# Prompt attention by pairs of heads, and a later gather of the sample values, in a hybrid decoder layer

## The chip, the cores and the metric

The kernel runs on one core of a Trainium2 chip. The metric is device time in microseconds (us) of one execution, the median over several runs; lower is better. The engines of the core are called PE (TensorE: matrix products, with PEld for its loads of the stationary operand), DVE (VectorE), ACT (ScalarE), POOL (GpSimd) and SP (SyncE, which here only issues DMAs). SBUF is the on-chip memory of 128 rows, PSUM the accumulators that PE writes.

## The reference, cut to what matters

One layer works on 1024 prompt tokens and on 8 samples of 4 tokens each (1056 columns in all). It projects the normalised input to queries, keys and values of 8 attention heads of width 64, to the inputs of a gated delta rule with 4 heads of width 128, and to two gates; it runs both branches, merges them under the gates, and ends with an MLP. The change touches the prompt part of this branch:

```
def stick_breaking(q, k, v, q_pos, k_pos, sb_bias):
    z = einsum('bqhd,bkhd->bhqk', q, k) * d ** -0.5 + sb_bias      # 8 heads, d = 64
    mask = k_pos[None, :] < q_pos[:, None]
    log_1m = where(mask, log_sigmoid(-z), 0)
    suffix = cumsum(log_1m, axis=3, reverse=True) - log_1m
    w = where(mask, exp(log_sigmoid(z) + suffix), 0)               # beta * product of (1 - beta) behind it
    return einsum('bhqk,bkhd->bqhd', w, v)
```

and, for the samples, the place where the pages of the cached keys and values (256 past tokens of each sample, two pages of 128) are gathered from a pool by a page table.

## The kernel before

**Products.** Results have to be exact to about fp32, and PE's fast format is float32r, so an operand is kept as a high and a low part. A dense product is three float32r products, of weights high by input high, weights high by input low, weights low by input high: lines L137, L138 and L139, wherever they appear. `tr` (L111) transposes a 128x128 block through PE.

**Order.** The program is written stage by stage, and a scheduler sets the order of each engine's instructions from its own simulated times. `tc.issue_after(x)` keeps what is written inside it behind instruction x, and `tc.high_priority()` lifts it ahead. Tiles come from pools with a number of buffers per tag; a PSUM tile is one bank of 128x512, from four pools: `dtile`, `gtile`, `ttile`, and a flag of `dtile` for a small fourth one.

**Stages.** Input projection and the prompt's delta-rule heads come first (0 to 520 us of the profile). Then the samples' delta rule (pool `dk`; it lies roughly at 545 to 600 us) and the samples' attention. From about 658 to 907 us comes the prompt's stick-breaking attention, and the MLP fills the rest.

**Sample keys and values.** For each sample s, `keys(s)` gathers two key pages into `kg` (L594, GpSimd's indirect DMA of 128 rows by 512 numbers) and transposes them on PE (`dkt`); `values(s)` gathers two value pages into `vg` (L607). They are called in turn for samples 0 to 3, ahead of the samples' delta rule. That rule multiplies keys and queries with the samples' stored states, two batches of 32 products into `dks` (L723: `sst` state against `kz` masked keys; each uses all rows and 32 columns of the array), and solves a small triangular system; `dMT` is its transposed matrix, `drk` (POOL, L114) a norm that `ds` (DVE, L702) needs. `dst` (L766) are the updates of the states.

**Prompt attention.** A block is one head `hh` and one tile `i` of 128 queries; it sees n = 128 (i+1) keys. For a head, `attn_load` puts q high into rows 0 to 63 and q low into rows 64 to 127 of `qs`, and key high twice into `kh`, key low twice into `kl`. The scores of a block are then two products of the whole array's 128 rows for each 512 keys, `sc<-kh,qs` (L932) and `sc<-kl,qs` (L933), which make all four of high by high, high by low, low by high and low by low. ACT's sigmoid (L934) empties PSUM into `s`; POOL masks the diagonal (L935) and forms `am` = 1 - s (L938); DVE makes the running product `pr` (L942) and multiplies (L943). PE transposes the weights (`wt<-ident,s`, L111), ACT copies them out (L954), and PE multiplies with the values: `po<-wt,vn` (L980 and L994), each with 64 columns of the array, so that 128 rows by 64 columns work. For heads 0 to 5 one `po` tile holds two query tiles of one head, one in each half of the columns, and ACT copies it to `oT` (L982), written out once per head. For heads 6 and 7 one `po` tile holds both heads, and its result stays in SBUF.

The pipeline runs blocks in order; at block x it issues the scores of block x + LAG (LAG = 4), then the transposes of block x (behind those scores by `issue_after`), then fill work, then the values of x. Fill work in the first SPLIT = 34 blocks is the gate projection `pd_g` and the residual's transposes `xrp`, and in the rest the products `pb` of the other branch. Heads 6 and 7 go from the longest block to the shortest.

Of the kernel before, what the change touches and what calls it, by code (L numbers as in the profile page):

```python
# [18 lines left out]
P = 128  # L19
D = 1024  # L20
NP = 1024
# [9 lines left out]
HD = 64  # L31
GH = 4
NC = NP // P
# [5 lines left out]
def hybrid_step(ctx, tc, x_prompt, x_sample, cache_k, cache_v, page_table, state_conv, state_ssm,  # L39
# [5 lines left out]
    V, S_, G, PE, SY = nc.vector, nc.scalar, nc.gpsimd, nc.tensor, nc.sync  # L45
# [132 lines left out]
    blk = keep.tile([P, 32, 4], F32, name="blk")  # L178
# [13 lines left out]
    for t in range(9):  # L192
        n = P if t < 8 else NS
# [9 lines left out]
        for hf in range(2):  # L203
            pt = (ttile, gtile)[hf](f"xtp{t}_{hf}")
# [374 lines left out]
    bk = pool("bk", stack=bctx, side="right")  # L579
    idx = bk.tile([P, 16], I32, name="idx")  # L580
# [6 lines left out]
    cvf = cache_v[0].rearrange("n t h d -> (n t) (h d)")  # L587

    vgs, kts_ = {}, {}
# [14 lines left out]
    def values(s):  # L604
        vgs[s] = bk.tile([P, 2, 512], F32, tag="vg", name=f"vg{s}", bufs=4)
        for pg in range(2):
            G.indirect_dma_start(vgs[s][:, pg, :], None, cvf, bass.IndirectOffsetOnAxis(ap=idx[:, 2 * s + pg:2 * s + pg + 1], axis=0))  # L607

    for s in range(4):
        keys(s)  # L610
        values(s)
    dctx = ExitStack()
    dk = pool("dk", stack=dctx, side="right")
    blkf = blk.rearrange("p b t -> p (b t)")
# [10 lines left out]
                    channel_multiplier=0)  # L625
# [14 lines left out]
    for b in range(3):  # L640
        pt = gtile(f"cvo{b}")
# [70 lines left out]
    pmt = gtile("dmt")  # L712
    tr(pmt[:, 0:P], dM)
    dMT = dk.tile([P, P], F32, name="dMT")
    V.tensor_copy(dMT, pmt[:, 0:P])
    pks = gtile("dks")
    for i, i0 in enumerate((4, 0)):
        kz = dk.tile([P, GH, NSEQ, NS], F32, tag="big", name=f"kz{i}")
# [2 lines left out]
        for s in range(NSEQ):  # L721
            for h in range(GH):
                PE.matmul(pks[32 * h:32 * h + 32, i * P:(i + 1) * P], lhsT=kz[:, h, s, :], rhs=sst[:, s, h, :],  # L723
                          start=(s == 0), stop=(s == NSEQ - 1))
# [6 lines left out]
    for it in range(3):  # L731
# [21 lines left out]
                           op0=ALU.mult, op1=ALU.mult)  # L753
# [8 lines left out]
    for hf in range(2):  # L762
        pts = [(gtile if h % 2 == 0 else ttile)(f"dst{h}{hf}") for h in range(GH)]
# [85 lines left out]
    for g in range(2):  # L849
# [5 lines left out]
        for s4 in range(4):  # L855
            s = 4 * g + s4
# [47 lines left out]

    actx = ExitStack()
    ak = pool("ak", 2, stack=actx, side="right")
    LAG = 4

    def attn_load(hh):
        p, a = hh // 2, hh % 2  # L910
        rs = slice(64 * a, 64 * a + 64)
        qs = ak.tile([P, NP], F32R, tag="qs", name=f"qs{hh}")
        kh = ak.tile([P, NP], F32R, tag="kh", name=f"kh{hh}")
        kl = ak.tile([P, NP], F32R, tag="kl", name=f"kl{hh}")

        for r in range(2):
            hs = slice(64 * r, 64 * r + 64)
            SY.dma_start(qs[hs].bitcast(F32), q_d[r][p, rs])
            SY.dma_start(kh[hs].bitcast(F32), k_d[0][p, rs])
            SY.dma_start(kl[hs].bitcast(F32), k_d[1][p, rs])  # L920
        return qs, kh, kl

    def scores(blk):
        hh, i = blk
        qs, kh, kl = heads[hh]
        n = P * (i + 1)
        qsl = slice(i * P, n)
        s = ak.tile([P, NP], F32, tag="s", name=f"s{hh}_{i}", bufs=LAG + 2)
        for k0 in range(0, n, 512):
            kn_ = min(512, n - k0)  # L930
            pt = dtile(f"sc{hh}_{i}_{k0}")
            PE.matmul(pt[:, :kn_], lhsT=qs[:, qsl], rhs=kh[:, k0:k0 + kn_], start=True, stop=False)  # L932
            last = PE.matmul(pt[:, :kn_], lhsT=qs[:, qsl], rhs=kl[:, k0:k0 + kn_], start=False, stop=True)  # L933
            S_.activation(s[:, k0:k0 + kn_], pt[:, :kn_], AF.Sigmoid, bias=sbb[:, hh:hh + 1], scale=HD ** -0.5)  # L934
        G.affine_select(s[:, qsl], s[:, qsl], pattern=[[-1, P]], compare_op=ALU.is_gt, fill=0.0, base=0,  # L935
                        channel_multiplier=1)
        am = ak.tile([P, NP], F32, tag="am", name=f"am{hh}_{i}", bufs=2)
        G.tensor_scalar(am[:, :n], s[:, :n], -1.0, 1.0, op0=ALU.mult, op1=ALU.add)  # L938

        pr = ak.tile([P, NP], F32, tag="pr", name=f"pr{hh}_{i}")  # L940
        am_r = am[:, n - 1:0:-1]
        V.tensor_tensor_scan(pr[:, n - 1:0:-1], am_r, am_r, 1.0, op0=ALU.mult, op1=ALU.bypass)  # L942
        V.tensor_tensor(s[:, :n - 1], s[:, :n - 1], pr[:, 1:n], op=ALU.mult)  # L943
        return s, last

    def transposed(blk, s):
        hh, i = blk
        wt = ak.tile([P, NP], F32, tag="wt", name=f"wt{hh}_{i}", bufs=2)
        for b0 in range(0, i + 1, 4):
            bn = min(4, i + 1 - b0)  # L950
            pt = ttile(f"wt{hh}_{i}_{b0}")
            for b in range(bn):
                tr(pt[:, b * P:(b + 1) * P], s[:, (b0 + b) * P:(b0 + b + 1) * P])
            S_.activation(wt[:, b0 * P:(b0 + bn) * P], pt[:, :bn * P], AF.Copy)  # L954
        return wt

    heads, vns, oTs, wts = {}, {}, {}, {}

    def load_v(p):
        vn = ak.tile([P, NC, P], F32, tag="vn", name=f"vn{p}", bufs=2)  # L960
        SY.dma_start(vn, v_d[p])
        return vn

    def values_of(blk):
        hh, i = blk
        p, a = hh // 2, hh % 2
        vn = vns[p]
        if hh < 6:
            if i % 2 == 0:
                return  # L970
            m = i // 2
            if m == 0:
                oTs[hh] = ak.tile([P, NC // 2, P], F32, tag="oT", name=f"oT{hh}")
            rs = slice(64 * a, 64 * a + 64)
            po = gtile(f"po{hh}_{m}")
            for b in range(2 * m + 2):
                for r in range(2):
                    if b > 2 * m + r:
                        continue
                    PE.matmul(po[64 * r:64 * r + 64, 0:P], lhsT=vn[:, b, rs], rhs=wts[hh, 2 * m + r][:, b * P:(b + 1) * P],  # L980
                              start=(b == 0), stop=(b == 2 * m + r))
            S_.activation(oTs[hh][:, m, :], po[:, 0:P], AF.Copy)  # L982
            if m == NC // 2 - 1:
                for r in range(2):
                    SY.dma_start(o_d[p, rs, 0:NP].rearrange("d (m r c) -> d r m c", r=2, c=P)[:, r],
                                 oTs[hh][64 * r:64 * r + 64])
            return
        if a == 0:
            return
        po = gtile(f"po6_{i}")  # L990
        for b in range(i + 1):
            for x in range(2):
                rs = slice(64 * x, 64 * x + 64)
                PE.matmul(po[rs, 0:P], lhsT=vn[:, b, rs], rhs=wts[6 + x, i][:, b * P:(b + 1) * P], start=(b == 0), stop=(b == i))  # L994
        cs_ = slice(i * P, (i + 1) * P)
# [3 lines left out]
    blks = [(hh, i) for hh in range(6) for i in range(NC)] + [(6 + a, i) for i in range(NC - 1, -1, -1) for a in range(2)]  # L999
    NB = len(blks)  # L1000
    SPLIT = 34
    state = {}

    def stage_a(x):
        if x >= NB:
            return
        hh, _ = blks[x]
        if hh not in heads:
            if hh // 2 not in vns:
                vns[hh // 2] = load_v(hh // 2)  # L1010
            heads[hh] = attn_load(hh)
        state[x] = scores(blks[x])

    def stage_b(x, fill):

        ahead = state[min(x + LAG, NB - 1)][1]
        with tc.issue_after(ahead.ins):
            wts[blks[x]] = transposed(blks[x], state[x][0])
        for f in fill:
            f()  # L1020
# [122 lines left out]
    pipeline(SPLIT, NB - 2, steps[:-6])  # L1143
    pipeline(NB - 2, NB, steps[-6:])
# [518 lines left out]
```

## Time and profile before

| what | value |
|---|---|
| median of 3 runs | 1745.47 us (1745.25 to 1745.96) |
| profiled execution | 1754.63 us, of which the span is 1752.9 us |
| granted TensorE clock, mean | 0.992 |
| PE busy | 1704.8 us, 97% of the span, 13902 products |
| DVE, ACT, POOL busy | 1148.9, 783.2, 206.6 us |

The profiled execution is 9.2 us longer than the median. Busy times in the views are of that execution. A row of a timeline gives start, duration, engine, line, operation, output and operands, array shape, and how often it runs in succession; a bracket gives the idle time before it and what ended it. Since products overlap in the pipeline, what one product costs is the distance from its start to the next start, and not its duration.

### The profile page before, as it was taken

The numbers are of one execution on the slowest core, as the hardware profiler recorded it, in microseconds if no ns is written. First come the engines' busy times: TensorE is split into PE (matmuls) and PEld (weight loads), VectorE is DVE, ScalarE is ACT, GpSimd is POOL, SyncE is SP. The second block draws the span as 40 slices with busy tenths as digits, with TensorE's granted clock in tenths as the row PEclk, the third lists the DMA queues.
The fourth block names the chain that finished last, engine by engine and source line by source line (L and its number), as shares of the span: only waits on it lengthen the run. The fifth ranks groups of instructions, "written<-read, shape, count | busy, mean of one in ns | idle before, by whom it ended". The sixth has DMA issues, their size and how long they took to land.

```text
span 1752.9 us, 34523 instructions
## 1 busy us (share of the span) xinstructions
PE 1704.8 (97%) x13902; PEld 1645.2 (94%) x13902; DVE 1148.9 (66%) x2299; ACT 783.2 (45%) x1554; POOL 206.6 (12%) x247
## 2 busy tenths in 40 slices
PE   7999999999998999999999999999999999999998
PEld 6999999999998787887989999999999999999998
DVE  6665677868224416658857487887777678788843
ACT  5553435343323225555433355554544564444353
POOL 1110111110004125335310000000000000000000
PEclk9999999999998999999999999999999999999999
DMA  5142232234337457758223644554443666532321
GB/s 177 37 127 67 67 117 79 81 96 144 118 97 230 138 161 210 188 145 248 67 86 117 194 126 146 164 150 148 146 150 133 212 215 220 170 123 90 128 83 66
DMA packets 234219, 239.22 MB, mean 136 GB/s; under 512 B 22882, under 2 KB 192195, under 8 KB 234060
## 3 DMA queue, kind: packets, MB, share of 16 engines
q1 hardware_dynamic: 229110, 226.27, 42.4%
q0 software_dynamic: 3200, 10.52, 1.9%
q8 instruction: 109, 1.79, 0.4%
q10 hardware_dynamic: 1750, 0.23, 0.1%
q14 instruction: 50, 0.41, 0.1%
HBM read 163.21 MB, written 73.77 MB: 135 GB/s over the span
## 4 chain that ended last, share of the span: by engine, by line
PE 74%; issue 8%; DMA 6%; DVE 6%; POOL 3%; ACT 1%; SPq 1%; POOLq 0%; DVEq 0%; ACTq 0%
PE pu L139 6%; PE pu L137 6%; PE pu L138 6%; PE pw L139 4%; PE pw L138 4%; PE pw L137 4%; PE pd_g L137 2%; POOL am L938 2%; PE pd_g L139 2%; PE pd_g L138 2%; POOL s L935 1%; PE px L138 1%; PE px L137 1%; PE px L139 1%; PE pv L137 1%
## 5 line engine op out<-in xcount | busy, mean ns | idle before, releaser
L139 PE MATMUL pu<-Xh,ul 128*128 128x264 f32 x812 | 230.1, 284 | 0.0
L137 PE MATMUL pu<-Xh,uh 128*128 128x264 f32 x812 | 229.8, 283 | 0.1
L138 PE MATMUL pu<-Xl,uh 128*128 128x264 f32 x812 | 229.7, 283 | 0.0
L137 PE MATMUL pw<-hc,w 128*128 128x264 f32 x728 | 205.4, 285 | 2.4 <-ACT w L1475 2.4
L138 PE MATMUL pw<-hc,w 128*128 128x264 f32 x728 | 205.7, 286 | 0.0
L139 PE MATMUL pw<-hc,w 128*128 128x264 f32 x728 | 200.9, 285 | 1.0 <-DVE w L1476 1.0
L137 PEld LDWEIGHTS pu<-Xh,uh 128*128 128x128 f32 x812 | 153.1, 189 | 0.3 <-ACT uh L1226 0.3
L137 PE MATMUL pd_g<-xh,wh_g 128*128 128x256 f32 (+1 forms) x512 | 150.9, 295 | 1.8 <-ACT gt L1037 1.6
L138 PEld LDWEIGHTS pu<-Xl,uh 128*128 128x128 f32 x812 | 152.7, 188 | 0.0
L139 PEld LDWEIGHTS pu<-Xh,ul 128*128 128x128 f32 x812 | 152.0, 188 | 0.0
L139 PE MATMUL pd_g<-xh,wl_g 128*128 128x256 f32 (+1 forms) x512 | 149.2, 291 | 0.1
L138 PE MATMUL pd_g<-xl,wh_g 128*128 128x256 f32 (+1 forms) x512 | 148.6, 290 | 0.0
L137 PEld LDWEIGHTS pw<-hc,w 128*128 128x128 f32 x728 | 137.9, 190 | 2.6 <-ACT w L1475 2.6
L138 PEld LDWEIGHTS pw<-hc,w 128*128 128x128 f32 x728 | 137.2, 189 | 0.0
L139 PEld LDWEIGHTS pw<-hc,w 128*128 128x128 f32 x728 | 134.4, 188 | 1.4 <-DVE w L1476 1.4
L942 DVE TENSOR_TENSOR_SCAN pr<-am 128x127 f32<-128x127 f32 (+7 forms) x64 | 88.1, 1378 | 54.8 <-POOL am L938 54.8
L137 PEld LDWEIGHTS pd_g<-xh,wh_g 128*128 128x128 f32 x512 | 97.8, 191 | 7.0 <-ACT gt L1037 3.0
L139 PEld LDWEIGHTS pd_g<-xh,wl_g 128*128 128x128 f32 x512 | 97.6, 191 | 2.0 <-issue 1.9
L138 PEld LDWEIGHTS pd_g<-xl,wh_g 128*128 128x128 f32 x512 | 97.6, 191 | 0.6 <-issue 0.4
L1475 ACT ACTIVATE w<-a 128x512 fp32r<-128x512 f32 x78 | 43.5, 620 | 84.5 <-PE pw L139 74.4
L139 PE MATMUL px<-mh,wl_wo 128*128 128x264 f32 x256 | 72.2, 285 | 0.9 <-DVE wl_wo L1227 0.8
L138 PE MATMUL px<-ml,wh_wo 128*128 128x264 f32 x256 | 72.6, 285 | 0.0
(584 smaller groups left out, 5126.2 us busy)
## 6 DMA issues: line engine op xcount, KB each, us to landing
hc_d<-t SPq DMA_DIRECT2D x26, 924.0 KB
hc<-hc_d SPq DMA_DIRECT2D x87, 264.0 KB
a<-in_w_down_dram SPq DMA_DIRECT2D x48, 256.0 KB
ws_g<-in_w_in_dram SPq DMA_DIRECT2D x16, 512.0 KB
ws_wo<-in_w_o_dram SPq DMA_DIRECT2D x32, 256.0 KB
ua<-in_w_up_dram SPq DMA_DIRECT2D x16, 512.0 KB
ub<-in_w_up_dram SPq DMA_DIRECT2D x16, 512.0 KB
gA_d<-gt SPq DMA_DIRECT2D x8, 528.0 KB
```

Source lines behind the costliest of these rows:

```text
L137: PE.matmul(pt[:, :n], lhsT=wh[k], rhs=xh[k], start=(k == 0), stop=False)
L138: PE.matmul(pt[:, :n], lhsT=wh[k], rhs=xl[k], start=False, stop=False)
L139: PE.matmul(pt[:, :n], lhsT=wl[k], rhs=xh[k], start=False, stop=(k == nk - 1))
L935: G.affine_select(s[:, qsl], s[:, qsl], pattern=[[-1, P]], compare_op=ALU.is_gt, fill=0.0, base=0, channel_multiplier=1)
L938: G.tensor_scalar(am[:, :n], s[:, :n], -1.0, 1.0, op0=ALU.mult, op1=ALU.add)
L942: V.tensor_tensor_scan(pr[:, n - 1:0:-1], am_r, am_r, 1.0, op0=ALU.mult, op1=ALU.bypass)
L1475: S_.activation(tl[:, 0], src, AF.Copy)
```

## The change

Two edits go together.

1. Prompt attention runs by pairs of heads. A block is a pair `p` and a query tile `i`. Keys high and low are loaded once for a pair, with one head in rows 0 to 63 and the other in 64 to 127; the queries are loaded per block (`q`, high and low, two DMAs). Scores of a head are three products (high by high, high by low, low by high) on that head's 64 rows, into a PSUM bank of its own; the two heads' products are written in turn. A `po` tile always holds both heads of one query tile, and moves from `gtile` to `ttile`; the results go out per block. LAG and SPLIT count pairs now: 2 and 17. `s` has 8 buffers instead of 6.
2. The gathers of the sample values for samples 0 to 3 are written behind the copy of `dMT`, and take their row numbers from `idxv`, a copy of `idx` that is made only after that.

```
-        values(s)                     # in the loop over samples, ahead of the delta rule
+    idxv = bk.tile([P, 16], I32, name="idxv")
...
+    mark = V.tensor_copy(dMT, pmt[:, 0:P])
+    with tc.issue_after(mark.ins):
+        V.tensor_scalar(idxv, idx, 0, None, op0=ALU.add)
+    for s in range(4):
+        values(s)
...
-            pt = dtile(f"sc{hh}_{i}_{k0}")
-            PE.matmul(pt[:, :kn_], lhsT=qs[:, qsl], rhs=kh[:, k0:k0 + kn_], start=True, stop=False)
-            last = PE.matmul(pt[:, :kn_], lhsT=qs[:, qsl], rhs=kl[:, k0:k0 + kn_], start=False, stop=True)
+            mk = dtile if k0 == 0 else gtile
+            pts = [mk(f"sc{p}_{i}_{k0}{a}") for a in range(2)]
+            for x, k_ in ((0, kh), (0, kl), (1, kh)):
+                for a in range(2):
+                    rs = slice(64 * a, 64 * a + 64)
+                    last = PE.matmul(pts[a][:, :kn_], lhsT=q[rs, x], rhs=k_[rs, k0:k0 + kn_],
+                                     start=(x == 0 and k_ is kh), stop=(x == 1))
...
+        po = ttile(f"po{p}_{i}")
+        for b in range(i + 1):
+            for a in range(2):
+                rs = slice(64 * a, 64 * a + 64)
+                PE.matmul(po[rs, 0:P], lhsT=vns[p][:, b, rs], rhs=wts[a][:, b * P:(b + 1) * P], ...)
+            S_.activation(o, po[:, 0:P], AF.Copy)
+            SY.dma_start(o_d[p, :, cs_], o)
...
         ahead = state[min(x + LAG, NB - 1)][1]
+        for a in range(2):
+            with tc.issue_after(ahead.ins):
+                wts[a] = transposed(blks[x], a, state[x][0][a])
+            for f in fill[:(len(fill) + 1) // 2] if a == 0 else fill[(len(fill) + 1) // 2:]:
+                f()
         values_of(blks[x])
```

What it does to the order is told by the engines' rows. On PE, in the prompt attention, before, where a block of one head (query tile 4) is scored; `sc_4_0` are its first 512 keys, `sc_4_512` the rest:

```order
L980 MATMUL po_2_7960<-wt_4_7884,vn_7635 64x128
L111 MATMUL wt_6_0_7985<-ident,s_6_7768 128x128 x4
L932 MATMUL sc_4_0_8067<-kh_7865,qs_7864 128x512
L980 MATMUL po_2_7960<-wt_5_7931,vn_7635 64x128 x2
L111 MATMUL wt_6_4_7991<-ident,s_6_7768 128x128 x3
L933 MATMUL sc_4_0_8067<-kl_7866,qs_7864 128x512
L932 MATMUL sc_4_512_8071<-kh_7865,qs_7864 128x128
L933 MATMUL sc_4_512_8071<-kl_7866,qs_7864 128x128
L137 MATMUL pd_g_6_0_8092<-xh_173,wh_g_6_8088 128x256
```

And in the changed program, also at query tile 4; `sc_4_00` is the first 512 keys of the first head of the pair, `sc_4_01` of the second:

```order
L937 MATMUL sc_4_00_7865<-kh_7637,q_4_7860 128x512
L937 MATMUL sc_4_00_7865<-kl_7638,q_4_7860 128x512
...
L137 MATMUL pd_g_5_2_7903<-xh_169,wh_g_5_7731 128x256
L138 MATMUL pd_g_5_2_7903<-xl_170,wh_g_5_7731 128x256
L937 MATMUL sc_4_01_7866<-kh_7637,q_4_7860 128x512
L937 MATMUL sc_4_01_7866<-kl_7638,q_4_7860 128x512
...
L139 MATMUL pd_g_5_2_7903<-xh_169,wl_g_5_7732 128x256
L111 MATMUL wt_11_0_7822<-ident,s_11_7674 128x128 x2
L978 MATMUL po_1_7852<-wt_10_7798,vn_7641 64x128
```

The third product of each head (again `kh`, with q low) stands behind the two that are shown. Two products of a head that the code writes in turn with the other head's come in a row here, with dense products between the heads.

On POOL, at the samples' delta rule, before, each row two gathers or one operation:

```order
L594 DMA kg_4302<-in_cache_k_dram,idx 128x512 x2
L607 DMA vg_4318<-in_cache_v_dram,idx 128x512 x2
L607 DMA vg_4337<-in_cache_v_dram,idx 128x512 x2
L607 DMA vg_4356<-in_cache_v_dram,idx 128x512 x2
L114 TENSOR_TENSOR drk<-drk_4434,powc 128x1
L594 DMA kg_4321<-in_cache_k_dram,idx 128x512 x2
L594 DMA kg_4340<-in_cache_k_dram,idx 128x512 x2
```

And in the changed program:

```order
L594 DMA kg_4299<-in_cache_k_dram,idx 128x512 x2
L114 TENSOR_TENSOR drk<-drk_4423,powc 128x1
L594 DMA kg_4315<-in_cache_k_dram,idx 128x512 x2
L594 DMA kg_4331<-in_cache_k_dram,idx 128x512 x2
L607 DMA vg_4478<-in_cache_v_dram,idxv 128x512 x2
L607 DMA vg_4481<-in_cache_v_dram,idxv 128x512 x2
```

The norm `drk` and the third and fourth samples' keys moved ahead of the values.

On PE at the same place, before, the first batch of `dks` is one row, between the transpose of dM and a gate projection:

```order
L111 MATMUL dmt<-ident,dM 128x128
L723 MATMUL dks<-sst,kz_4489 32x128 x32
L138 MATMUL pd_g_3_1_7108<-xl_172,wh_g_3_7078 128x256
L139 MATMUL pd_g_3_1_7108<-xh_171,wl_g_3_7079 128x256
L137 MATMUL pd_g_3_1_7108<-xh_171,wh_g_3_7078 128x256
```

And in the changed program:

```order
L111 MATMUL dmt<-ident,dM 128x128
L727 MATMUL dks<-sst,kz_4491 32x128 x5
L111 MATMUL dkt_0_4319<-ident,kg_4315 128x128
L727 MATMUL dks<-sst,kz_4491 32x128 x3
L111 MATMUL dkt_1_4325<-ident,kg_4315 128x128
L727 MATMUL dks<-sst,kz_4491 32x128 x9
L111 MATMUL dkt_0_4319<-ident,kg_4315 128x128 x3
L111 MATMUL dkt_1_4325<-ident,kg_4315 128x128 x3
L727 MATMUL dks<-sst,kz_4491 32x128 x15
```

The transposes of the third sample's keys came in among the batch.

More of the change, by code (lines that the diff above doesn't have):

```diff
@@ L606, in values @@
         for pg in range(2):
-            G.indirect_dma_start(vgs[s][:, pg, :], None, cvf, bass.IndirectOffsetOnAxis(ap=idx[:, 2 * s + pg:2 * s + pg + 1], axis=0))
+            G.indirect_dma_start(vgs[s][:, pg, :], None, cvf, bass.IndirectOffsetOnAxis(ap=idxv[:, 2 * s + pg:2 * s + pg + 1], axis=0))
     for s in range(4):
         keys(s)
-        values(s)
+    idxv = bk.tile([P, 16], I32, name="idxv")
     dctx = ExitStack()
@@ L906, in hybrid_step @@
     ak = pool("ak", 2, stack=actx, side="right")
[L907 to L921, printed above, removed]
+    LAG = 2
@@ L923, in scores, with load_pair @@
+    def load_pair(p):
+        kh = ak.tile([P, NP], F32R, tag="kh", name=f"kh{p}")
+        kl = ak.tile([P, NP], F32R, tag="kl", name=f"kl{p}")
+        SY.dma_start(kh.bitcast(F32), k_d[0][p])
+        SY.dma_start(kl.bitcast(F32), k_d[1][p])
+        return kh, kl
     def scores(blk):
-        hh, i = blk
-        qs, kh, kl = heads[hh]
+        p, i = blk
+        kh, kl = heads[p]
         n = P * (i + 1)
         qsl = slice(i * P, n)
-        s = ak.tile([P, NP], F32, tag="s", name=f"s{hh}_{i}", bufs=LAG + 2)
+        q = ak.tile([P, 2, P], F32R, tag="q", name=f"q{p}_{i}", bufs=4)
+        for x in range(2):
+            SY.dma_start(q[:, x].bitcast(F32), q_d[x][p, :, qsl])
+        s = [ak.tile([P, NP], F32, tag="s", name=f"s{p}_{i}{a}", bufs=8) for a in range(2)]
@@ new lines, in scores @@
+            for x, k_ in ((0, kh), (0, kl), (1, kh)):
[4 more added lines that the diff above has]
+            for a in range(2):
+                S_.activation(s[a][:, k0:k0 + kn_], pts[a][:, :kn_], AF.Sigmoid, bias=sbb[:, 2 * p + a:2 * p + a + 1],
+                              scale=HD ** -0.5)
@@ new lines, in scores @@
+        for a in range(2):
+            G.affine_select(s[a][:, qsl], s[a][:, qsl], pattern=[[-1, P]], compare_op=ALU.is_gt, fill=0.0, base=0,
+                            channel_multiplier=1)
+            am = ak.tile([P, NP], F32, tag="am", name=f"am{p}_{i}{a}", bufs=2)
+            G.tensor_scalar(am[:, :n], s[a][:, :n], -1.0, 1.0, op0=ALU.mult, op1=ALU.add)
+            pr = ak.tile([P, NP], F32, tag="pr", name=f"pr{p}_{i}{a}")
+            am_r = am[:, n - 1:0:-1]
+            V.tensor_tensor_scan(pr[:, n - 1:0:-1], am_r, am_r, 1.0, op0=ALU.mult, op1=ALU.bypass)
+            V.tensor_tensor(s[a][:, :n - 1], s[a][:, :n - 1], pr[:, 1:n], op=ALU.mult)
@@ L955, in transposed @@
         return wt
-    heads, vns, oTs, wts = {}, {}, {}, {}
+    heads, vns, wts = {}, {}, {}
     def load_v(p):
@@ L1006, in stage_a @@
             return
[L1007 to L1011, printed above, removed]
+        p, _ = blks[x]
+        if p not in heads:
+            heads[p] = load_pair(p)
+            vns[p] = load_v(p)
         state[x] = scores(blks[x])
@@ L1016, in stage_b @@
         ahead = state[min(x + LAG, NB - 1)][1]
[L1017 to L1020, printed above, removed]
+        for a in range(2):
+            with tc.issue_after(ahead.ins):
+                wts[a] = transposed(blks[x], a, state[x][0][a])
+            for f in fill[:(len(fill) + 1) // 2] if a == 0 else fill[(len(fill) + 1) // 2:]:
+                f()
         values_of(blks[x])
@@ L1142, in hybrid_step @@
     steps = [lambda j=j, c=c, f=(x == 0): pb_step(j, c, f) for j in range(KT) for x, c in enumerate(range(4))]
-    pipeline(SPLIT, NB - 2, steps[:-6])
-    pipeline(NB - 2, NB, steps[-6:])
+    pipeline(SPLIT, NB - 1, steps[:-6])
+    pipeline(NB - 1, NB, steps[-6:])
     ofa = []
```

58 lines of the change are left out of this document (12 added, 46 removed).

## The prediction

> **What bounds the kernel now.** I read the page first (engines), then the stretches of the two stages that the change touches, then PE's timeline inside them, the groups of the attention stage, and last the waits of POOL and DVE at the delta rule. Columns of the stretches: us, busy us (count) of PE, PEld, DVE, ACT, POOL, then granted clock, DMA share, GB/s.
>
> ```profile
> PE 1704.8 (97%) x13902; PEld 1645.2 (94%) x13902; DVE 1148.9 (66%) x2299; ACT 783.2 (45%) x1554; POOL 206.6 (12%) x247
> ...
> 550.00:560.00 10.00, 8.10 (x93) 6.84 (x91) 3.38 (x14) 5.49 (x12) 7.97 (x9) 0.97 0.93 292
> 560.00:570.00 10.00, 7.59 (x44) 5.91 (x43) 1.31 (x2) 0.38 (x1) 2.64 (x3) 0.51 0.39 109
> 570.00:580.00 10.00, 10.00 (x121) 8.40 (x120) 4.27 (x6) 2.56 (x5) 4.82 (x4) 1.00 0.30 89
> 700.00:760.00 60.00, 59.80 (x502) 53.66 (x503) 33.67 (x32) 32.87 (x73) 18.24 (x30) 1.00 0.70 187
> 760.00:850.00 90.00, 86.80 (x675) 74.16 (x675) 67.01 (x65) 48.41 (x101) 42.49 (x46) 1.00 0.65 183
> 850.00:910.00 60.00, 60.00 (x518) 53.57 (x518) 36.10 (x57) 24.41 (x54) 12.23 (x25) 1.00 0.12 34
> ```
>
> In the prompt attention (700 to 910) PE is busy 206.6 of 210 us, DVE at most three quarters of a stretch. PE is the bound there, so what the change does to PE's stream goes into the end almost one to one. At the samples' delta rule PE is the engine that waits: 4.3 us idle in 550 to 570, and a granted clock of 0.51 in the second half of it.
>
> **Scores: the stream.** Distances between starts give what one product costs.
>
> ```profile
> 702.40 0.39 PE L933 MATMUL sc<-kl,qs 128*128 128x512 f32 x1
> 702.63 0.40 PE L932 MATMUL sc<-kh,qs 128*128 128x512 f32 x1
> ...
> 706.17 0.28 PE L138 MATMUL pd_g<-xl,wh_g 128*128 128x256 f32 x1
> 706.29 0.28 PE L139 MATMUL pd_g<-xh,wl_g 128*128 128x256 f32 x1
> 706.50 0.43 PE L980 MATMUL po<-wt,vn 128*64 128x128 f32 x2
> 706.87 0.33 PE L932 MATMUL sc<-kh,qs 128*128 128x128 f32 x1
> 707.03 0.27 PE L933 MATMUL sc<-kl,qs 128*128 128x128 f32 x1
> 707.23 1.09 PE L980 MATMUL po<-wt,vn 128*64 128x128 f32 x12
> 708.25 0.76 PE L111 MATMUL wt<-ident,s 128*128 128x128 f32 x5
> ```
>
> 512 wide: 0.23 us (702.40 to 702.63). 256 wide: 0.12 (706.17 to 706.29). 128 wide: 0.11 (707.03 to 707.23 is 0.20, less 0.09 for leaving, below). 384 wide, between its neighbours: 0.175, an estimate. Before there are 96 products of 512 and 32 each of 384, 256 and 128: 96 x 0.233 + 32 x (0.175 + 0.119 + 0.109) = 35.4 us. After there are 144 and 48 each, half again as many. No row before shows products on 64 rows side by side in two halves of the rows. One bound is that none go side by side: 53.1 us. The other is that every pair does: 26.5 us. The nearest row is the x12 of po, two halves of the columns: 12 products in 1.02 us less 0.14 for a change is 0.88, eight steps of 0.11 and not twelve, so where neighbours in the queue use different halves, they overlap, and where they use the same half, they don't. I therefore go by the changed program's order. There the 288 products stand in 59 runs; 40 of them hold one head only (162 products, 31.2 us one after another), 19 hold both (126 products, 21.9 us one after another, 14.3 us with each pair of neighbours of different heads overlapped). 31.2 + 14.3 = 45.4. **Term: +10.0 us** (ends -8.9 and +17.7).
>
> **Changes of the array's shape.** Whenever products on part of the array follow products on the whole, or the reverse, the stream stops for a moment. The nearest rows with row tiles are the state updates on 32 rows among the gate products:
>
> ```profile
> 591.27 0.29 PE L137 MATMUL pd_g<-xh,wh_g 128*128 128x288 f32 x1
> 591.40 0.29 PE L138 MATMUL pd_g<-xl,wh_g 128*128 128x288 f32 x1
> 591.63 1.13 PE L766 MATMUL dst<-vexp,dkp 32*128 32x512 f32 x4
> 592.69 0.40 PE L139 MATMUL pd_g<-xh,wl_g 128*128 128x288 f32 x1
> 592.92 0.29 PE L137 MATMUL pd_g<-xh,wh_g 128*128 128x288 f32 x1
> ```
>
> A gate product of 0.13 us takes 0.23 when 32-row work is next (591.40 to 591.63), and again 0.23 when it comes first behind it (592.69 to 592.92): 0.10 each. The same for column halves: 0.21 instead of 0.12 from a gate product to po (706.29 to 706.50), 0.09. Two po products then take 0.37 instead of 0.22 (706.50 to 706.87): 0.09 for leaving and 0.06 for a first load that nothing covers. So a change costs 0.14 to 0.20 us, drain and first load together. Counted in the order: before, 132 changes (66 into po, 66 out of it; scores use the whole array and cost none of their own), 20.2 us. After, 206 (59 into score runs, 101 out of them to whole-array products or to po, 46 out of po), 34.9 us. **Term: +14.7 us** (ends: 0, if neighbours cover it, since the price is seen before only beside other shapes; +16, at 0.2 and 0.02 for each fragment).
>
> **Values.** 576 products either way. By the same step rule (neighbours in different halves overlap), 42.4 us before and 38.5 after, because both heads always alternate now. **Term: -3.9 us** (ends -6 and 0).
>
> **Waits of the attention.** The chain of a block is scores, sigmoid, mask, scan, transposes, copy, values.
>
> ```profile
> L980 PE MATMUL po<-wt,vn 128*64 128x128 f32 x432 | 42.0, 281 | 0.1
> L932 PE MATMUL sc<-kh,qs 128*128 128x512 f32 x48 | 21.2, 445 | 0.4 <-ACT s L934 0.2
> L954 ACT ACTIVATE wt<-wt 128x512 f32<-128x512 f32 x48 | 28.0, 596 | 18.4 <-PE wt L111 16.9 <-PE po L980 1.0
> ```
>
> The idle columns of po (0.1) and scores (0.4) show that the chain is hidden now; by pairs the slack from scores to transposes grows, because LAG 2 pairs is as many heads as LAG 4 before and fill work is spread as before. Only at the end, where the pair's blocks 3 to 0 come with little fill left, transposes, the 0.6 us copy and the values stand closer than copy plus drain (five places, 0.1 to 0.5 us apart where about 1.1 is needed): 3 to 5 us. Against it, the wait on DMA of the residual's rows and of the other branch in this stage can shrink by up to 2, since PE gets there later. The queries' 64 DMAs are new on SP's queue; they stand 13 to 33 us ahead of their use by the neighbours' times, three of them 3 to 7 us, which still covers a transfer of 64 KB; if not, 1 to 2 us. Copies of results per block add 24 small ACT and SP steps, under ACT's half-free time (32.87 busy of 60). **Term: +2 us** (ends 0 and +7).
>
> **The delta rule.**
>
> ```profile
> 555.39 1.28 PE L723 MATMUL dks<-sst,kz 128*32 128x128 f32 x34
> 557.28 0.43 PE L723 MATMUL dks<-sst,kz 128*32 128x128 f32 x4 [0.61 <-issue]
> 558.71 0.43 PE L723 MATMUL dks<-sst,kz 128*32 128x128 f32 x4 [1.00 <-issue]
> ...
> 565.06 0.58 PE L138 MATMUL pd_g<-xl,wh_g 128*128 128x256 f32 x1
> 565.44 0.42 PE L139 MATMUL pd_g<-xh,wl_g 128*128 128x256 f32 x1
> 565.66 0.42 PE L137 MATMUL pd_g<-xh,wh_g 128*128 128x256 f32 x1
> ...
> 572.13 1.51 PE L723 MATMUL dks<-sst,kz 128*32 128x128 f32 x46
> ...
> 556.73 0.94 POOL L607 DMA_INDIRECT vg<-in_cache_v_dram,idx  x1 [0.30 <-issue]
> 557.69 0.60 POOL L114 TENSOR_TENSOR drk<-drk,powc 128x1 f32<-128x1 f32 x1
> 558.32 0.16 DVE L702 TENSOR_TENSOR ds<-drk,db__4439 128x1 f32<-128x1 f32 x1 [4.38 <-issue]
> q8 instruction: 109, 1.79, 0.4%
> ```
>
> The first batch takes 9.67 us (555.39 to 565.06). The second ran 46 in 1.51 us, so 64 would take 2.1: a stall of 7.6 us, in which PE waits for nothing that the profile names. Behind it the gate products stand 0.22 apart instead of 0.12 (565.44 to 565.66), at the clock of 0.51: some 20 products to the end of that stretch, 2.0 us. Together 9.6 us. What it is can't be read off; what coincides is the DMA load (0.93 of the engines in 550 to 560, with eight value gathers, against 0.30 when the second batch ran fast) and that PE's instructions themselves arrive by DMA (109 packets over the span on a queue of their own). Removed are eight gathers ahead of this point; the norm drk no longer stands behind them, which ends DVE's 4.38 us wait. The four gathers of samples 2 and 3's keys come forward into their place, and the eight value gathers, 1.25 us apart, follow at about 557 to 568, in which nothing of PE needs the values (the samples' attention comes past 600). I take all but one gap like that at 558.71 (1.0 us): **-8.5 us** (ends -9.6 and +1, the second batch meeting the gathers). POOL has nothing urgent queued behind them.
>
> The Trainium skill ("Runtime: NRT & Kernel Launch", Instruction fetch mechanics) says that instructions come in blocks of 256 by the engine's own DMA queue and that crossing into the next is "mostly hidden". By that page this stall would not be the fetch's, and the term would be 0, the second rival below; no run here shows which yet.
>
> **Sum.** +10.0 + 14.7 - 3.9 + 2.0 - 8.5 = +14.3 us on the profiled execution's 1754.6, so 1768.9 with a profile. That execution stands 9.2 above the median; carrying the difference over, 1745.5 + 14.3 = **1759.8 us**.
>
> **Rivals.**
> - *Halves overlap everywhere (faster).* PE keeps both heads' products running even where a run holds several of one head, or the chip's order differs. Stream 26.5: 1759.8 - 18.9 = 1741 us. It decides from the point where 15 of the 18.9 us come, that is where nearly every product is covered. For it speaks that half the rows are free while one head runs; against it the x12 row, in which neighbours on the same half cost a full step, and dense products between the heads. The Trainium skill ("TensorEngine Tiling (Array Packing)", Theoretical Speedup) gives "up to 2×" for a dimension of 64 or less; by that page the stream would be this rival's.
> - *The stall stays, or isn't in unprofiled runs.* It is tied to no instruction that the change removes, it may move to the second batch, and 9.2 us between profile and median leave room for it to be the profile's own. Then the term is 0: 1768 us.
> - *Changes of shape are cheap for 64-row scores.* The price at half or nothing: 1745 to 1753 us. Against it the rows at 591.63 and 592.92.
> - *No overlap at all.* The three products of two heads stand one after another, 53.1: 1759.8 + 7.7 = 1767.5 us.
>
> **Chances.** A difference under 0.2% (3.5 us) is about what measurement can't tell from none. Forecast (1752 to 1764) 0.46; stall stays 0.25; cheap changes 0.14; no overlap 0.07; overlap everywhere 0.08. Faster takes the last and a little of the cheap changes, 0.11; the same takes most of the cheap changes and the low edge of the forecast, 0.12; slower the rest, 0.77. The range 1746 to 1771 leaves out the overlap rival (0.08), half of the cheap changes (0.07) and 0.05 above, where no overlap and a staying stall meet.
>
> **What the profile after would show.** Runs of sc on 64 rows whose starts are 0.23 apart for one head and 0.12 on average where heads alternate; a gate product of 0.21 ahead of and behind each run; the attention stage 20 us or so longer with PE still busy over 97%; dks in under 4 us and a clock of 1.0 in 560 to 570. A stage no longer than before, or sc starts 0.12 apart within one head's run, would prove the sum wrong.

## The result, and the profile after

The changed kernel takes 1770.2 us (median of 4, 1768.3 to 1774.3), against 1745.7 for the kernel before in the same comparison: ratio 1.0143, 95% interval 1.0123 to 1.0162, or 24.5 us slower. The forecast was 1759.8, slower, with a range up to 1771. The profiled execution took 1768.3 us, span 1766.5; that is 13.6 us above the profiled span of before, against a forecast of 14.3. The two comparisons differ because the profiled execution of before held a stall that its timed runs, by experiments 1 and 2, did not.

The engines' row of the page, and the stretches, with the same columns as before:

```profile
PE 1718.7 (97%) x13998; PEld 1647.7 (93%) x13998; DVE 1154.4 (65%) x2300; ACT 783.3 (44%) x1554; POOL 216.3 (12%) x247
...
560.00:570.00 10.00, 10.00 (x167) 8.79 (x166) 2.31 (x2) 2.56 (x5) 7.87 (x8) 1.00 0.69 198
570.00:580.00 10.00, 8.81 (x71) 8.41 (x70) 5.78 (x9) 1.89 (x4) 6.95 (x7) 1.00 0.74 206
...
850.00:910.00 60.00, 60.00 (x512) 53.40 (x512) 32.77 (x49) 22.68 (x47) 11.52 (x22) 1.00 0.09 26
```

PE is the bound as before, with 96 products more. At the delta rule it is busy all of 560 to 570 at a clock of 1.00, although the DMA share is 0.69. The timeline of PE there shows `dks` without a gap in which PE waits for nothing:

```profile
558.88 0.62 PE L727 MATMUL dks<-sst,kz 128*32 128x128 f32 x10
...
562.12 1.07 PE L727 MATMUL dks<-sst,kz 128*32 128x128 f32 x30
563.12 0.39 PE L138 MATMUL pd_g<-xl,wh_g 128*128 128x256 f32 x1
...
566.95 1.96 PE L727 MATMUL dks<-sst,kz 128*32 128x128 f32 x64
```

The first batch, with eight transposes of keys inside it, took 4.2 us (558.88 to 563.12; the prediction's sign was under 4). The second batch of 64 took 1.96 us, while the eight value gathers were being issued (559.97 to 570.97 on POOL). In the attention, a run of scores of one head looks like this:

```profile
711.09 0.49 PE L937 MATMUL sc<-kh,q 64*128 64x512 f32 x1
711.42 0.39 PE L937 MATMUL sc<-kl,q 64*128 64x512 f32 x1
711.66 0.39 PE L937 MATMUL sc<-kh,q 64*128 64x512 f32 x1
711.98 0.39 PE L137 MATMUL pd_g<-xh,wh_g 128*128 128x256 f32 x1
712.21 0.28 PE L138 MATMUL pd_g<-xl,wh_g 128*128 128x256 f32 x1
712.33 0.28 PE L139 MATMUL pd_g<-xh,wl_g 128*128 128x256 f32 x1
```

Three products of 512 take 0.89 us to the next start. The first costs 0.33 instead of 0.23 (its load lies open, 0.10), the last 0.32 (drain, 0.09), and the gate product behind it 0.23 instead of 0.12 (its load again, 0.11). The waits of PE in the stage, in us, times and the longest:

```profile
PE pb L137 <- DVE tb L1129: 3.3, 2, 2.2
PE wt L111 <- ACT wt L962: 1.4, 3, 0.6
```

They are small, as forecast, though the largest is one that the forecast did not have: `pb` waits for DVE to empty its PSUM tile.

### The profile page after: what moved, and what is told of

Its sections match the earlier page's. It is cut to its first block, busy times and chain, and to the rows that moved or that the text cites. A ratio compares the mean times of both kernels' runs of the same rounds, so it can differ in the third digit from the quotient of the medians.

```text
span 1766.5 us, 34813 instructions
## 1 busy us (share of the span) xinstructions
PE 1718.7 (97%) x13998; PEld 1647.7 (93%) x13998; DVE 1154.4 (65%) x2300; ACT 783.3 (44%) x1554; POOL 216.3 (12%) x247
## 4 chain that ended last, share of the span: by engine, by line
PE 82%; DMA 6%; DVE 6%; ACT 2%; issue 2%; POOL 1%; SPq 0%; DVEq 0%; POOLq 0%; ACTq 0%
PE pu L139 6%; PE pu L137 6%; PE pu L138 6%; PE pw L137 5%; PE pw L138 5%; PE pw L139 5%; PE pd_g L137 3%; PE pd_g L139 3%; PE pd_g L138 3%; PE sc L937 2%; PE po L978 2%; PE wt L111 2%; PE px L138 1%; PE px L137 1%; PE px L139 1%
## 5 line engine op out<-in xcount | busy, mean ns | idle before, releaser
L950 DVE TENSOR_TENSOR_SCAN pr<-am 128x127 f32<-128x127 f32 (+7 forms) x64 | 92.8, 1455 | 60.9 <-POOL am L946 60.9
L962 ACT ACTIVATE wt<-wt 128x512 f32<-128x512 f32 (+3 forms) x96 | 46.9, 491 | 59.0 <-PE wt L111 58.8
```

## Experiments

Each comparison ran beside the kernel before. Between the jobs, the kernel before itself took 1745 to 1747 us in some and 1753 to 1756 us in others; what goes with it is shown below, and only ratios are compared across jobs.

**1. The gathers alone.** The kernel before, with these lines (cut; the gathers read `idxv` instead of `idx`):

```
-        values(s)
+    with tc.issue_after(mark.ins):
+        V.tensor_scalar(idxv, idx, 0, None, op0=ALU.add)
+    for s in range(4):
+        values(s)
```

> The kernel before, with the second edit alone (value gathers of samples 0 to 3 behind the copy of dMT). Theory A, the 9.6 us stall at dks belonged to the one profiled execution and not to the runs that were timed: no change, 1745 to 1747 us, and a profile without the stall. Theory B, the stall is in every execution of the kernel before and the edit removes it: 1737 us (1745.5 - 8.5). Theory C, the gathers only move it to the second batch of dks: 1745 to 1747 as well, but with idle time at the second batch in the profile.

Measured: 1746.7 us against 1746.8, ratio 1.0002 (0.9992 to 1.0013). Its profile has no stall at either batch; the second, which theory C had in doubt, ran through with the gathers late:

```profile
563.12 1.95 PE L727 MATMUL dks<-sst,kz 128*32 128x128 f32 x64
```

That leaves theory A. A second time, later:

> The kernel before with the second edit alone, once more, on the chip that runs next. So far the stretch of PE's stream from product 4290 to 5184 took about 103 us where the profile shows no stall, 112 to 116 where it does with the gathers early, and 119 to 122 where it does with the gathers late. Theory A (the stall comes with some chips and executions, and the late gathers make it longer): where the kernel before takes 1744 to 1748 us, no difference; where it takes over 1750, 4 to 6 us slower, 0.3%. Theory B (the late gathers change nothing in either): within 0.1% in any case.

Measured: 1743.2 us against 1745.2, ratio 0.9987 (0.9973 to 1.0001). The edit gives no gain of 8.5 us (0.5%) in the timed runs. The second job was one with 1745 us for the kernel before, so it said nothing on theory A's other half.

**2. The pairs alone.** The changed kernel, with `values(s)` back in its place.

> The changed kernel with the first edit alone (attention by pairs; the gathers stand as before). Theory A: the whole loss is the pairs': 1770 us, as the changed kernel. Theory B, where the gathers' edit saves 8.5 us in every run: 1779 us.

Measured: 1767.0 us against 1746.8, ratio 1.0127 (1.0102 to 1.0151): the loss is the pairs'. Its profile, with the gathers early, has no stall either:

```profile
559.12 1.96 PE L723 MATMUL dks<-sst,kz 128*32 128x128 f32 x64
```

**3. The kernel before, profiled once more.**

> The kernel before, unchanged, for a second profile. Theory A (the 9.6 us stall at dks was an accident of that one execution): dks takes 2 to 3 us, the span is 1741 to 1746 us. Theory B (profiling or the program brings it each time): dks takes over 9 us again, span 1751 to 1754.

Measured: 1757.4 us, span 1755.7, in a job in which the timed runs of before had a median of 1756.4. The first batch of `dks` ran through, but PE starved a few us earlier, among `dkk` and the gate products. PE's timeline, with idle time and what ended it:

```profile
552.18 0.38 PE L137 MATMUL pd_g<-xh,wh_g 128*128 128x256 f32 x1 [0.43 <-issue]
...
554.32 0.38 PE L139 MATMUL pd_g<-xh,wl_g 128*128 128x256 f32 x1 [1.04 <-issue]
556.48 0.37 PE L139 MATMUL pd_g<-xh,wl_g 128*128 128x256 f32 x1 [0.85 <-issue]
```

And in a kernel with the late gathers, of the same job (experiment 7):

```profile
562.66 0.40 PE L727 MATMUL dks<-sst,kz 128*32 128x128 f32 x3 [0.99 <-issue]
...
565.51 1.09 PE L727 MATMUL dks<-sst,kz 128*32 128x128 f32 x4 [1.02 <-issue]
567.66 1.10 PE L727 MATMUL dks<-sst,kz 128*32 128x128 f32 x4 [1.06 <-issue]
```

So neither theory holds as it was put. The stall comes with the job: all six profiles of the two jobs with 1753 to 1756 us show it, five with late gathers and this one with early ones, and none of seven profiles of the jobs with 1745 to 1747 does, whether the gathers are early or late. The first profile of before is the one exception, a single execution with the stall beside timed runs of 1745. It is not the chip: one and the same chip ran a job of each kind. The stall lies at some 550 to 575 us, and not always at `dks`; in these profiles PE is idle in it for 4.2 to 6.4 us, waiting for nothing that the profile names.

Whether the late gathers make it longer stayed open. The stretch from product 4290 to product 5184 of PE's stream, which ends ahead of the prompt attention, took 102 to 104 us in the seven profiles without the stall, 113 and 116 us in the two of the kernel before with it, and 116 to 127 us in the five with late gathers and the stall. The ratios of such jobs below (the second part of experiment 6, and 7 to 10) set late gathers against early ones, so some of what they show can be this.

**4. Both heads' scores in one tile, heads in turn.** The PSUM tile of 512 keys holds both heads in two banks, so that both come free together, and each product is ordered behind the one before it:

```
-            pts = [mk(f"sc{p}_{i}_{k0}{a}") for a in range(2)]
+            pp = PS['p'].tile([P, 2, 512], F32, tag="d" if k0 == 0 else "g", ...)
+            pts = [pp[:, a, :] for a in range(2)]
...
+                    with tc.issue_after(last.ins), tc.high_priority():   # from the second product on
                         last = PE.matmul(...)
```

> The changed kernel, but the two heads' scores of 512 keys share one PSUM tile of two banks, and each product is ordered behind the one before it, so that the heads alternate: in the order 40 runs of scores instead of 59, nearly all alternating; changes of shape 178 instead of 206. Theory A (neighbours of different heads overlap, neighbours of one head don't, a change costs 0.14 to 0.20): stream 26.5 instead of 45.4, 28 changes fewer, 4.8 us: 1770 - 18.9 - 4.8 = 1746 us, and alternating pairs 0.23 us apart at 512 keys in the profile. Theory B (64-row products never overlap): the stream stays 53.1 us, 1765 to 1770. Theory C (one-head runs cost no more than mixed ones, all the loss is in the changes of shape): 1770 - 4.8 = 1765 us.

Measured: 1748.2 us against 1746.8, ratio 1.0005 (0.9993 to 1.0018): theory A's 1746 within 2 us, and far from the 1765 and more of theories B and C. Of the loss of 1.43%, 0.05% is left. A run in its timeline:

```profile
707.82 0.50 PE L955 MATMUL sc<-kh,q 64*128 64x512 f32 x2
708.16 0.40 PE L955 MATMUL sc<-kl,q 64*128 64x512 f32 x2
708.40 0.40 PE L955 MATMUL sc<-kh,q 64*128 64x512 f32 x2
708.73 0.39 PE L148 MATMUL pd_g<-xh,wh_g 128*128 128x256 f32 x1
```

Six products of two heads take 0.91 us, where one head's three took 0.89: the other half is free. The busy time of the 512-wide products in the stage, first in the changed kernel and then in this one:

```profile
L937 PE MATMUL sc<-kh,q 64*128 64x512 f32 x96 | 34.5, 438 | 0.0
L937 PE MATMUL sc<-kl,q 64*128 64x512 f32 x48 | 16.8, 400 | 0.0
```

```profile
L955 PE MATMUL sc<-kh,q 64*128 64x512 f32 x96 | 20.9, 439 | 0.0
L955 PE MATMUL sc<-kl,q 64*128 64x512 f32 x48 | 9.5, 391 | 0.0
```

51.3 us became 30.4 because both heads now stand in each run; the durations of single products hardly changed (438 and 439 ns, 400 and 391 ns).

**5. The same with the gathers early.**

> The kernel with the common PSUM tile and the heads in turn, but the sample values' gathers stand where they stood before: the first edit in its cheapest form, alone. Theory A: within 0.2% of the kernel before on any chip (1.0005 was measured with late gathers on a chip without the stall), and so 4 to 6 us faster than its twin with late gathers where the kernel before takes over 1750 us. Theory B: 1.005, as two other kernels with the common tile and late gathers on such a chip.

Measured: 1747.5 us against 1745.2, ratio 1.0012 (0.9996 to 1.0027): level with before, as in experiment 4. This job too was one with 1745 us for the kernel before, so theory B was not put to the test.

**6. One head behind the other.** First in the changed kernel with separate banks:

```
-            for x, k_ in ((0, kh), (0, kl), (1, kh)):
-                for a in range(2):
+            for a in range(2):
+                for x, k_ in ((0, kh), (0, kl), (1, kh)):      # each behind the last
```

> The changed kernel with each head's three products ordered one behind the other, first one head, then the other; in the order 65 runs of scores, 54 of them of one head, and 217 changes of shape instead of 206. Theory A: stream 50.1 instead of 45.4, 11 changes more, 1.9 us: 1770 + 4.7 + 1.9 = 1777 us. Theory B (no overlap in any case): only the 11 changes, 1772. Theory C: 1772.

Measured: 1770.9 us against 1746.8, ratio 1.0141 (1.0126 to 1.0157), less than theory A's 1777 and in line with the 1772 of theories B and C: putting the heads one behind the other costs next to nothing here (the attention stage took 282 us in its profile, 280 in the changed kernel's). Then the same two lines in the kernel with the common tile, where only the order inside a run differs:

> The kernel with the common PSUM tile of two banks, but each head's three products in a row instead of the heads in turn; runs (40) and changes of shape (180 against 178) stay as they are there, so only the order inside a run differs. Theory A (neighbours overlap only if they are of different heads): of six products in a run two neighbours in the middle overlap, five steps instead of three, stream 44.2 instead of 26.5: 17.7 us slower than with the heads in turn, 1748 + 18 = 1766 us where the kernel before takes 1747. Theory C (halves overlap whatever the order): no difference, 1748.

Measured: 1762.4 us against 1753.5, ratio 1.0052 (1.0035 to 1.0069), which no theory had. The profile tells more. A run in which the program has three products of one head and then three of the other (the trace gives a product's operands and not its head, so the order is taken from the program):

```profile
733.27 0.50 PE L955 MATMUL sc<-kh,q 64*128 64x512 f32 x2
733.60 0.40 PE L955 MATMUL sc<-kl,q 64*128 64x512 f32 x2
733.83 0.40 PE L955 MATMUL sc<-kh,q 64*128 64x512 f32 x2
734.16 0.39 PE L150 MATMUL pd_g<-xh,wl_g 128*128 128x256 f32 x1
```

The products start two by two, so those of the second head run beside those of the first, and the run takes 0.89 us; theory A wanted five steps, some 1.4. The 512-wide scores' busy time is 21.2 and 9.6 us, as with the heads in turn. So theory C is right about the order, but only within a run: in the changed kernel, where most runs hold one head, the time is lost. From the gate product ahead of the first score to behind the last value the stage took 261 us in both kernels. So the 0.5% (8.9 us) lies outside the stage. Ahead of it this job has the stall; the stretch of experiment 3 took 122.7 us here, 6 to 10 us more than in the kernel before with the stall:

```profile
560.00:570.00 10.00, 4.87 (x33) 1.54 (x32) 0.00 (x0) 0.60 (x1) 6.31 (x7) 0.67 0.72 207
```

**7. In turn, but each head in a bank of its own.** As 4, without the common tile.

> The changed kernel with the products of the two heads ordered in turn, one behind the other, but each head still in a PSUM bank of its own: the first product goes alone when its bank comes free, the other five alternate behind it. In the order 66 runs, 224 changes of shape, stream 34.0 instead of 45.4. Theory A: 1770 - 11.4 + 18 x 0.17 = 1762 us: between the changed kernel and the one with the common bank. Theory D (changes are free): 1759. Theory B (no overlap): 1773.

Measured: 1774.4 us against 1756.4, ratio 1.0100 (1.0074 to 1.0126). Carried to 1746, that is 1763: theory A's 1762, within the interval (1759 to 1768); theory B's 1773 lies outside, theory D's 1759 at the edge. This job has the stall, so the stage itself says more: 273.1 us in its profile, 6.8 less than in the changed kernel (279.9). Theory A's sum has 8.3 less, theory D's 11.4 less, theory B's 3 more.

**8. Two products instead of three.**

```
-            for x, k_ in ((0, kh), (0, kl), (1, kh)):
+            for x, k_ in ((0, kh), (0, kl)):
```

> The changed kernel without the third product of each head (query low by key high is left out): 192 products on 64 rows instead of 288. In the order 67 runs of scores and 219 changes of shape (206 in the changed kernel), stream 31.4 us instead of 45.4 where only different heads overlap. Theory A: 1770 - 14.0 + 13 x 0.17 = 1758 us; the 12 us that remain above the kernel before are then changes of shape and waits, since the stream itself is shorter than before. Theory C (all of the loss is in the changes): 1772 us. Theory D (the loss is the third product's stream alone and changes are free): 1744 us or less.

Measured: 1777.3 us against 1756.4, ratio 1.0105 (1.0075 to 1.0135). Carried to 1746 that is 1764, between 1759 and 1769: a little above theory A's 1758, under theory C's 1772 and far from theory D's 1744. Here the scores are no more numerous than before (192), and the kernel is still 1% slower. Two products of one head in its timeline:

```profile
734.48 0.49 PE L937 MATMUL sc<-kh,q 64*128 64x512 f32 x1
734.82 0.39 PE L937 MATMUL sc<-kl,q 64*128 64x512 f32 x1
735.14 0.39 PE L137 MATMUL pd_g<-xh,wh_g 128*128 128x256 f32 x1
735.36 0.28 PE L138 MATMUL pd_g<-xl,wh_g 128*128 128x256 f32 x1
```

0.66 us for two, and 0.22 for the product behind them, against 0.23 a product for the whole-array scores of before and 0.12 for a gate product: a run of two pays some 0.3 us for its changes of shape. How much of the 1% is theirs was not separated from the stall of this job and from a lower clock: the profile, of the slowest of the four runs, has a mean clock of 0.95 in the stage, against 0.99 in the changed kernel's.

**9. Whole-array scores in the schedule of pairs.** The changed kernel with the scores of before: q high and low stacked, keys doubled, two products. With them `s` has 6 buffers instead of 8, and the keys 3 instead of 2.

> The changed kernel (both edits), but the scores go back to the form of before: query high and low stacked in 128 rows, keys doubled, two whole-array products a head (192 in all, no change of shape of their own); pairs, LAG 2, the common po tile and the late gathers stay. Keys have 3 buffers, s has 6. Theory A (the loss is the score stream and the score runs' changes of shape, and the pair's po tile is a gain): stream as before, changes 100 instead of 132, 32 x 0.17 = 5.4 us, values 4.0 us less, waits 2 more: 1746 - 7.4 = 1739 us. Theory B (the pair schedule itself loses time, by the bare last blocks or the keys' loads): 1746 us or more, with idle time on PE in the profile's last blocks.

Measured: 1780.1 us against 1756.4, ratio 1.0131 (1.0109 to 1.0154): theory A missed by far. The PE waits of its stage:

```profile
PE sc L943 <- DMA q<-qh_d: 5.0, 1, 5.0
PE wt L111 <- ACT wt L967: 4.3, 4, 2.7
PE pb L137 <- DVE tb L1134: 4.0, 5, 1.4
PE pd_g L137 <- ACT xs L1045: 2.8, 2, 1.5
```

With doubled keys of two heads and four small query loads a block on SP, the first scores waited 5.0 us for q, and shorter waits added up; the mean clock in the stage was 0.95 as well. Theory B's time (1746 or more) is met, though the longest wait is at the first scores and not in the last blocks. It does not show that pairs as such lose: in the changed kernel the first scores waited 0.6 us for q, `wt` 1.4 and `pb` 3.3.

**10. More distance.** As 4, with LAG 3 instead of 2.

> The kernel with the common PSUM tile and the heads in turn, with LAG 3 instead of 2: 35 runs of scores instead of 40, 168 changes of shape instead of 178, one more block of distance between scores and transposes. Theory A (changes of shape cost 0.14 to 0.20, and the last blocks' waits shrink with the distance): 1.7 us for the changes and about 2 for the waits, 1744 us where the kernel before takes 1747: 0.2% faster, if at all. Theory B (the last blocks wait for the copy between transposes and values, whatever LAG is): 1746 to 1748, with the same waits in the profile.

Measured: 1762.6 us against 1753.5, ratio 1.0056 (1.0036 to 1.0076), as its neighbour in the same job (experiment 6). The wait for the copy at the last blocks is there still (2.6 us at its longest), and its stage took 263 us against 261 in experiment 4, so theory B holds for the waits; like its neighbour's, its profile has the stall, so the 0.5% can't be put down to LAG. No version here beats the kernel before beyond its interval.

## Why the prediction was right or wrong, point by point

The direction and the range held; of 24.5 us, 14.3 were forecast. The table sets the attention stage of the two profiles without a stall side by side: gathers alone against pairs alone. It is made of the distances between PE's starts in their timelines, grouped by what stands there; the drain is what the last step ahead of a change takes beyond the product's own price.

| part of the stage, us | gathers alone | pairs alone | difference | forecast |
|---|---|---|---|---|
| scores' stream | 38.5 | 45.0 | +6.5 | +10.0 |
| drains at changes of shape | 12.1 | 21.3 | +9.2 | with the next |
| whole-array products, open loads in them | 147.9 (1203) | 160.4 (1244) | +12.5, of which 41 x 0.123 = 5.0 are products that moved into the stage: +7.5 | +14.7 with the drains |
| values' stream | 43.9 | 39.9 | -4.0 | -3.9 |
| idle | 8.5 | 8.9 | +0.4 | +2 |

The sum is 19.6 us; the spans differ by 1764.0 - 1740.6 = 23.4. The 3.8 between lie ahead of the stage, which starts 4.4 us later in pairs alone (651.4 against 647.0); 3.6 of that is there at product 4290 already (541.5 against 537.9), which comes at 536.7 to 541.5 in all the profiles here.

Two things have to be known to set this table beside the forecast. The row of the scores' stream holds the open first loads of the score runs: at 0.10 each (less for 128 keys), 5.4 us in pairs alone and 1.8 in gathers alone, which the forecast counts among the changes of shape. And pairs alone has an order of its own: by the starts, 31 of its 58 score runs hold one head only, against 40 of 59 in the changed kernel.

- **Scores' stream, +10.0:** the right kind, 3.5 us too high. Without first loads and drains, the changed kernel's own profile has 31.1 us in the 40 one-head runs (31.2 in the prediction) and 12.7 in the 19 mixed ones (14.3); gathers alone has 37.3 (35.4 in the prediction). That is +6.5. The reading that neighbours overlap only if they are of different heads was wrong in its reason: by experiment 6, order within a run does not count. What counts is whether a run holds both heads. The sum came near because 40 of 59 runs hold one head, where both readings agree.
- **Changes of shape, +14.7:** too low. The two rows of the table have 16.7 us, and with the first loads of the score runs (5.4 - 1.8) it is 20.3, of which the lower mean clock in the stage of pairs alone (0.988 against 0.993) may be 1.4, an estimate. The price of 0.14 to 0.20, taken from 32-row products and from `po`, held for 64-row scores, by the rows at 711.09 to 712.33, and the rival of cheap changes falls with it; what else lies above the forecast sits in the row of the whole-array products and was not followed further.
- **Values, -3.9:** -4.0 measured.
- **Waits, +2:** +0.4 of idle; the bare last blocks cost little, and the wait for `tb` was not foreseen.
- **Delta rule, -8.5:** this is the step that failed. The stall was real in the profiled execution, and absent in the one after, so the profiles' difference (13.6) met the forecast. That was luck: the stall does not go with this edit, and the two terms above were off by 3.5 and 5.6 us in opposite directions. And the timed runs of before had no such stall (experiments 1 and 2), so nothing was there to be saved. The second rival, that the stall is not in the unprofiled runs, gave 1768 and decided the size. The warning was in the forecast's own numbers: a profiled execution 9.2 us above the median, and a stall of 9.6.
- **The rival of overlap everywhere** became true by another program: with both heads in every run the kernel comes to 1.0005, against 1.0143 for the changed one. The changed kernel lost by the scheduler's order: with a bank for each head, most runs hold one head, and the common tile ended that (experiment 4), while ordering the heads in turn with separate banks ended it in part (experiment 7). The Trainium skill's figure of "up to 2×" ("TensorEngine Tiling (Array Packing)", Theoretical Speedup) is met inside such a run, 0.91 us for six products against 0.89 for three; the trace agrees where both tiles have work at once, and not where they don't.

## What to carry to other kernels

Half-array products pay only if the other half has work in the same unbroken run: give both halves' results one tile, so that they come free together, and count the runs in the order before counting products. Each run among whole-array work cost about 0.4 us beyond its stream here (two drains of 0.09, two open loads of 0.10 and 0.11), so by this price few long runs should beat many short ones. And compare the profiled execution with the timed median before costing a stall that the profile shows: if it stands above the median by as much as the stall, the stall may be that execution's own, as it was here.

## What was not expected of the hardware

Two half-array streams run past each other: with three products of one half ahead in the program's order, the run's second product started 0.01 us behind its first and the six took three steps, so the other half did not wait for the third (experiment 6). PE can be idle for 4 to 6 us around one place of its stream with no wait that the profile shows, in some jobs and not in others on the same kernel; early and late gathers both have it and both go without it, and its cause stays open.

And idle time can be paid twice. Behind the 2.2 us wait for `tb` in the changed kernel, the granted clock fell, with PE busy 96% of the stretch (the clock is the third number from the end):

```profile
830.36 0.61 PE L137 MATMUL pb<-obh,wh_pb 128*128 128x288 f32 x1 [2.23 <-DVE tb L1129]
...
830.00:840.00 10.00, 9.64 (x68) 8.79 (x68) 6.59 (x7) 3.37 (x6) 3.99 (x4) 0.83 0.30 107
```

It is no rule. Behind a wait of nearly the same length in pairs alone the clock stayed at 1.00:

```profile
566.45 0.41 PE L111 MATMUL dkt<-ident,kg 128*128 128x128 f32 x2 [2.11 <-DMA kg<-in_cache_k_dram,idx]
...
560.00:570.00 10.00, 7.89 (x127) 6.82 (x120) 1.86 (x5) 1.47 (x3) 5.92 (x8) 1.00 0.61 199
570.00:580.00 10.00, 10.00 (x91) 9.27 (x90) 6.69 (x8) 2.94 (x5) 5.41 (x5) 1.00 0.55 141
```

What decides between the two was not found.
